# First expert matrix: VectorE and GpSimd in program order, with paced routing

## The chip, the cores and the metric

The kernel runs on one core of a Trainium2 chip. The metric is the device time of one execution in microseconds; the median of three runs before the change is 2098.88 us (2098.55 to 2100.28). The engines are named as in the profile: PE (TensorE), DVE (VectorE), ACT (ScalarE), POOL (GpSimd), SP (the DMA queues of SyncE).

## The reference, cut to what matters

Two transformer blocks for 256 tokens of width 1024. The change lies in the expert layer of the first block, which retrieves 16 single-neuron experts out of 128 x 128 for each of 8 heads:

```python
qh = (x_blk @ w_q).reshape(tc, PEER_HEADS, 2, PEER_HALF)
scores = jnp.einsum('thpc,hpnc->thpn', qh, skf)
s_top, i_top = lax.top_k(scores, PEER_TOPK)
cand = s_top[:, :, 0, :, None] + s_top[:, :, 1, None, :]
...
c_s, c_pos = lax.top_k(cand.reshape(tc, PEER_HEADS, PEER_TOPK * PEER_TOPK), PEER_TOPK)
g = jax.nn.softmax(c_s, axis=-1)
u = expert_u[e_idx]
v = expert_v[e_idx]
a = jax.nn.gelu(jnp.einsum('td,thkd->thk', x_blk, u), approximate=False)
return jnp.einsum('thk,thkd->td', g * a, v)
```

The kernel gathers nothing. It computes the product of every token with all 16384 rows of `expert_u` (the first matrix), and multiplies the result by gates that are zero for experts not chosen, before the product with `expert_v`.

## The kernel before, in words

**Order of the stages.** A projection gives the queries (`s_mode` over `w_q`, 16 steps), and each group of 4 of its output tiles is followed by the scores against the sub-keys (`q_evac`). Then `u_part(0, ...)` computes blocks 0 to 63 of the first matrix (128 experts each), `u_part(64, ...)` blocks 64 to 127, and two `v_part` calls the product with the second matrix. While the second half of the first matrix runs, the gates of the first half are built and applied; the gates of the second half run beside `v_part`.

**One block of the first matrix.** `blocks(j)` (line 760) takes the raw block, which a stream has loaded into one of 4 buffers, and transposes it on DVE (line 767) in two parts: the larger into an SBUF tile `ut` (640 columns for j < 64, else 768), the rest into a PSUM tile. `parted(j)` (line 770) splits the result into a rounded high part and the remainder: ACT copies both parts into `uhi` (line 774), then POOL subtracts for the larger part and DVE for the smaller (line 776, `ulo`). The tiles `whi`, `wlo` and `ut` have 3 buffers each. PE runs 24 matmuls per block (lines 247 to 249: eight chunks, three products), and ACT applies the Gelu (line 794). In `u_part` the split runs two blocks ahead of PE and the transpose three ahead.

**Routing.** The generator `chosen` loads and transposes the sub-keys (`sub_keys`), searches the best 16 of 128 scores 32 times (`tops`, `best`, lines 849 to 855: MAX8, FIND_INDEX8 and MATCH_REPLACE8 on DVE), then for each half of the tokens builds 64 candidate sums, searches 8 times in them, decodes positions and picks the indices by comparison (`routing`, lines 864 to 955; the pick steps are lines 912 to 921). Each `yield` is a place where the caller may go on with its own work. The query stage advances it by two yields per step (line 971 ff.), `u_part(0)` by 2.3 yields per block through `every`.

**Gates.** `hot(i)` (line 996) makes the one-hot tiles of 8 tokens: two comparisons (lines 1008 and 1011) and two products (line 1010) on DVE. `outer(i)` (line 1013) runs 16 small matmuls into PSUM (line 1018), `apply(i)` (line 1021) multiplies the expert results by them (line 1024, two instructions). `pipe(..., fine=True)` runs these three for 32 groups as three yields per step, and `u_part(64)` advances it by 1.7 yields per block.

**What sets the order.** Outside a `manual_schedule` block the framework's scheduler orders each engine's instructions when the program is built, starting from program order and letting what is ready go ahead. Inside such a block the named engines keep program order. Before the change neither half of the first matrix stands in such a block. Loads of raw blocks are issued from SP, ACT and, for j < 64, POOL (line 102). Waits between engines are semaphores that the framework places.

Of the kernel before, what the change touches and what calls it, by code (L numbers as in the profile page):

```python
# [9 lines left out]
F32 = mybir.dt.float32  # L10
# [4 lines left out]
ALU = mybir.AluOpType  # L15
# [141 lines left out]
def tile_kernel(ctx: ExitStack, tc: tile.TileContext, I, out, cst, dbg=None):  # L157
# [186 lines left out]
    adv = [0.0]  # L344

# [409 lines left out]
    with ExitStack() as pp:  # L755
# [14 lines left out]
        def parted(j, tr):  # L770
            hi = wpool.tile([P, D], F32R, tag="whi", name=f"uhi{j}", bufs=3)
            lo = wpool.tile([P, D], F32R, tag="wlo", name=f"ulo{j}", bufs=3)
            for _, c, x in tr:
                S.activation(hi[:, c], x, AF.Copy)  # L774
            for eng, c, x in tr:
                eng.tensor_tensor(lo[:, c], x, hi[:, c].bitcast(F32), op=ALU.subtract)  # L776
            return hi, lo

        def u_part(j0, trs, dst, bg, n):
# [18 lines left out]
            drain(bg)  # L798

        with ExitStack() as pr_:  # L800
# [58 lines left out]
            def tops(q):  # L859
                for e in range(4 * q, 4 * q + 4):  # L860
                    for t in range(2):
                        yield from best(top[t][:, e], ti[t][:, e], sco[t][:, e, :], e % 2)

            def routing():
# [3 lines left out]
                for t in range(2):  # L868
# [14 lines left out]
                    yield  # L883
                    for h in range(8):
                        yield from best(cs[:, h], cp[:, h], cand[:, h], True)
# [9 lines left out]
                    yield  # L895
# [3 lines left out]
                    yield  # L899
# [3 lines left out]
                    yield  # L903
# [3 lines left out]
                    yield  # L907
                    ix = R.tile([P, 2, P], F32, tag="ix", name=f"ix{t}")

                    for s in range(2):  # L910
# [3 lines left out]
                        yield  # L914
                        V.tensor_tensor(e, e, tf[:, s, :, None, :].to_broadcast([P, 16, 16, 8]), op=ALU.mult)
                        yield
                        V.tensor_tensor(e[:, 0:8], e[:, 0:8], e[:, 8:16], op=ALU.add)
                        yield
# [3 lines left out]
                        yield  # L922
                    for _ in range(3):
                        yield
# [4 lines left out]
                    yield  # L929
                    for s in range(2):  # L930
                        V.tensor_copy(ixt[s][:, ts], ps[:, s * P:(s + 1) * P])

# [6 lines left out]
                for _ in range(6):  # L939
                    yield  # L940
                V.tensor_reduce(sm, g, axis=AX.X, op=ALU.add)
                yield
# [3 lines left out]
                for _ in range(3):  # L946
                    yield
# [3 lines left out]
                yield  # L951
                V.tensor_scalar(ixt[2], ps[:, :T], GS, None, op0=ALU.mult)
                yield
                V.scalar_tensor_tensor(ixt[3], ps[:, :T], GS, ixt[2], op0=ALU.mult, op1=ALU.subtract)
                yield

            def chosen():
                yield from sub_keys()
                yield
# [32 lines left out]
        def gates(half, dst, H):  # L992
# [34 lines left out]
            yield from pipe(T // 8, (1, outer), (2, apply), (0, hot), fine=True)  # L1027
# [24 lines left out]
        with tc.tile_pool(name="hot", bufs=1) as H:  # L1052
            bgg = gates(0, a0, H)
            u_part(64, ahead, a1, bgg, 1.7)
# [6 lines left out]
            bgg = gates(1, a1, H)  # L1061
# [455 lines left out]
```

## Time and profile before

| what | value |
|---|---|
| median of three runs | 2098.88 us |
| profiled execution, its own time | 2100.21 us |
| its span | 2098.4 us |
| PE busy | 2015.3 us (96%) |
| DVE busy | 1484.0 us (71%) |
| ACT busy | 907.0 us (43%) |
| POOL busy | 448.3 us (21%) |
| mean granted clock of PE | 0.986 of full speed |

A busy PE is not a PE at its best: matmuls are pipelined, so the count of instructions in a stretch says more than the busy time. In the rows of windows further down, a row is a stretch, its length, and then for each of PE, PEld (weight loads), DVE, ACT and POOL the busy time and in brackets the number of instructions; behind them the granted clock, the DMA share and GB/s. Rows of a timeline are start, duration, engine, line, operation, tile written and tiles read; a bracket at the end is idle time before it and what ended it. Rows of waits are who waited for whom, the sum in us, how often, and the longest. Rows of groups are line, engine, operation, shapes and count, then the busy sum and the mean in ns of one.

### The profile page before, as it was taken

What the parts mean: (1) busy time and instruction counts of PE and PEld (TensorE: products, weight loads), DVE (VectorE), ACT (ScalarE), POOL (GpSimd) and SP (SyncE); (2) the same over time, 40 slices, a digit from 0 to 9 for tenths busy, and PEclk for the clock granted to TensorE, in tenths of its full rate; (3) what the DMA queues carried; (4) which work ended last, traced back from release to release, by engine and by line L of the source; (5) the groups of instructions that cost most, each with busy time, mean ns of one, the idle gap of its engine ahead of it and who ended that gap; (6) DMA issues with size and microseconds to landing.
All of it is one profiled execution on the core that took longest, in us unless ns stands there. A gap on an engine that the chain in (4) does not pass through costs nothing.

```text
span 2098.4 us, 33634 instructions
## 1 busy us (share of the span) xinstructions
PE 2015.3 (96%) x12513; PEld 1747.3 (83%) x12513; DVE 1484.0 (71%) x2664; ACT 907.0 (43%) x1537; POOL 448.3 (21%) x458
## 2 busy tenths in 40 slices
PE   8999998999999999999999998999999989899999
PEld 7898987999999888878887777877888878558997
DVE  4666699779999888879667758756532377766554
ACT  4565543544333444444454223322222267565443
POOL 0002665764455300010002211111000033300000
PEclk9999999999999999999999999999999999999999
DMA  6435564775555644468557645456532345115654
GB/s 221 141 121 194 159 161 131 195 176 139 137 142 141 201 161 158 157 226 292 194 186 243 216 158 186 157 190 218 176 101 90 119 141 157 52 61 151 181 186 146
DMA packets 181032, 344.18 MB, mean 164 GB/s; under 512 B 18412, under 2 KB 87684, under 8 KB 180868
## 3 DMA queue, kind: packets, MB, share of 16 engines
q1 hardware_dynamic: 138388, 254.44, 39.8%
q0 software_dynamic: 20512, 67.53, 10.3%
q10 hardware_dynamic: 21968, 20.06, 3.4%
q8 instruction: 98, 1.61, 0.3%
q14 instruction: 66, 0.54, 0.1%
HBM read 339.78 MB, written 2.18 MB: 163 GB/s over the span
## 4 chain that ended last, share of the span: by engine, by line
PE 69%; issue 10%; DVE 10%; POOL 5%; DMA 5%; ACT 1%; SPq 0%; POOLq 0%; DVEq 0%; ACTq 0%
PE acc L279 9%; PE acc L278 9%; PE acc L280 9%; PE acc L1045 5%; PE acc L1046 5%; PE acc L1049 5%; PE acc L312 4%; PE acc L313 4%; PE acc L315 4%; POOL ulo L776 4%; DMA mem<-in_mod_w_dram 2%; PE acc L249 2%; PE acc L247 2%; PE acc L248 2%; PE misc L1018 2%
## 5 line engine op out<-in xcount | busy, mean ns | idle before, releaser
L109 DVE TENSOR_TENSOR wlo<-raw,whi 128x1024 fp32r<-128x1024 f32 (+2 forms) x401 | 483.7, 1209 | 399.4 <-ACT whi L108 396.3
L108 ACT ACTIVATE whi<-raw 128x1024 fp32r<-128x1024 f32 (+1 forms) x412 | 429.8, 1046 | 660.5 <-PE acc L279 276.2
L278 PE MATMUL acc<-act,whi 128*128 128x512 f32 (+1 forms) x944 | 322.4, 343 | 3.1 <-DVE act L1089 3.1
L280 PE MATMUL acc<-act,wlo 128*128 128x512 f32 (+1 forms) x944 | 321.7, 341 | 2.6 <-DVE wlo L109 2.6
L279 PE MATMUL acc<-act,whi 128*128 128x512 f32 (+1 forms) x944 | 322.7, 342 | 1.6 <-DVE act L1090 1.6
L249 PE MATMUL acc<-x2h,ulo 128*128 128x256 f32 x1024 | 296.0, 289 | 17.7 <-DVE ulo L776 14.2
L247 PE MATMUL acc<-x2h,uhi 128*128 128x256 f32 x1024 | 294.8, 288 | 2.9 <-DVE ulo L776 2.5
L248 PE MATMUL acc<-x2l,uhi 128*128 128x256 f32 x1024 | 291.5, 285 | 0.0
L776 POOL TENSOR_TENSOR ulo<-ut,uhi 128x640 fp32r<-128x640 f32 (+1 forms) x128 | 224.3, 1763 | 162.1 <-ACT uhi L774 156.6
L249 PEld LDWEIGHTS acc<-x2h,ulo 128*128 128x128 f32 x1024 | 198.2, 194 | 25.0 <-DVE ulo L776 17.7
L278 PEld LDWEIGHTS acc<-act,whi 128*128 128x128 f32 x944 | 180.3, 192 | 31.0 <-DVE act L1089 4.0
L247 PEld LDWEIGHTS acc<-x2h,uhi 128*128 128x128 f32 x1024 | 198.6, 194 | 4.8 <-DVE ulo L776 4.8
L1045 PE MATMUL acc<-whi,g 128*128 128x512 f32 x512 | 202.6, 396 | 0.0
L1046 PE MATMUL acc<-wlo,g 128*128 128x512 f32 x512 | 199.9, 390 | 0.9 <-DVE wlo L109 0.9
L280 PEld LDWEIGHTS acc<-act,wlo 128*128 128x128 f32 x944 | 181.2, 192 | 22.8 <-DVE wlo L109 3.0
L279 PEld LDWEIGHTS acc<-act,whi 128*128 128x128 f32 x944 | 181.1, 192 | 21.5 <-DVE act L1090 2.4
L248 PEld LDWEIGHTS acc<-x2l,uhi 128*128 128x128 f32 x1024 | 198.3, 194 | 0.0
L774 ACT ACTIVATE uhi<-ut 128x640 fp32r<-128x640 f32 (+1 forms) x128 | 101.5, 793 | 223.8 <-DVE ut L767 169.7
L1049 PE MATMUL acc<-whi,g 128*128 128x512 f32 x512 | 157.8, 389 | 0.0
L496 DVE SCALAR_TENSOR_TENSOR mem<-mem,silu_c 128x1024 f32<-128x1024 f32 x84 | 106.5, 1281 | 18.9 <-DMA mem<-in_mod_w_dram 18.6
L767 DVE STREAM_TRANSPOSE ut<-raw 128x640 f32<-128x640 f32 (+1 forms) x128 | 114.5, 894 | 6.1 <-DMA raw<-in_peer_u_dram 3.7
L1046 PEld LDWEIGHTS acc<-wlo,g 128*128 128x128 f32 x512 | 96.2, 188 | 21.0 <-DVE wlo L109 2.3
(397 smaller groups left out, 3816.3 us busy)
## 6 DMA issues: line engine op xcount, KB each, us to landing
raw<-in_peer_v_dram SPq DMA_DIRECT2D x128, 512.0 KB, 3.3
raw<-in_peer_u_dram SPq DMA_DIRECT2D x320, 128.0 KB, 3.3
mem<-in_mod_w_dram POOLq DMA_DIRECT2D x64, 512.0 KB, 5.3
raw<-in_ffn_w_down_dram SPq DMA_DIRECT2D x50, 512.0 KB, 3.2
raw<-in_ffn_w_gate_dram SPq DMA_DIRECT2D x44, 512.0 KB, 4.4
raw<-in_ffn_w_up_dram SPq DMA_DIRECT2D x44, 512.0 KB, 3.8
raw<-in_w_in_dram SPq DMA_DIRECT2D x40, 512.0 KB, 3.8
raw<-in_peer_u_dram ACTq DMA_DIRECT2D x128, 128.0 KB, 3.4
```

The source lines that it names most:

```text
L108: a = self.nc.scalar.activation(hi, src, AF.Copy)
L109: b = (eng or self.nc.vector).tensor_tensor(lo, src, hi.bitcast(F32), op=ALU.subtract)
L247: mm(ps, lh, rh, start=first, stop=False)
L248: mm(ps, lh, rl, start=False, stop=False)
L249: mm(ps, ll, rh, start=False, stop=last)
L278: mm(ps[n][:, cs], hi[:, k - k0, c], xh[:, k, cs], start=first, stop=False)
L279: mm(ps[n][:, cs], hi[:, k - k0, c], xl[:, k, cs], start=False, stop=False)
L280: mm(ps[n][:, cs], lo[:, k - k0, c], xh[:, k, cs], start=False, stop=last)
L776: eng.tensor_tensor(lo[:, c], x, hi[:, c].bitcast(F32), op=ALU.subtract)
L1045: mm(ov[t][h], gh[:, ts], vh[:, 0, hs], start=j == 0, stop=False)
L1046: mm(ov[t][h], gh[:, ts], vl[:, 0, hs], start=False, stop=False)
L1049: mm(ov[t][h], gl[:, ts], vh[:, 0, hs], start=False, stop=j == P - 1)
```

## The change

- Both halves of the first matrix stand in a block that keeps DVE and POOL in program order. The first covers `u_part(0)` and the transposes of blocks 64 and 65, the second `u_part(64)`.
- In `u_part` a block first takes a piece of background work (routing or comparisons), then transposes block j+3, then splits block j+2, then takes late background work. POOL's subtraction gets a wait for the last DVE instruction ahead of the transposes (`latest`, `mark`).
- All blocks are divided 768 to 256 between POOL and DVE.
- Routing yields an estimated cost in us, and `budget` lets so much of it pass per call: 3.4 per step of the query stage from the fifth step on, 1.25 per block. A bare `yield` ends the current slice. The sub-keys are loaded in the first four steps, five yields each.
- The gates' three parts are called separately: `hot` ahead of the transposes in even blocks (twice in the first), `outer(i)` and `apply(i-1)` behind the split in odd ones. The gates of the second half keep `pipe`.

The diff, cut to its core:

```diff
+    def budget(per, gen):
+        due = per
+        for cost in gen:
+            due = min(due - cost, per) if cost else min(due, 0.0)
+            while due <= 0:
+                yield
+                due += per
...
-            c = (5 if j < 64 else 6) * P
+            c = 6 * P
...
+        def latest():
+            return next(i for i in reversed(nc.cur_bb.bb.instructions) if i.engine == V.engine)
...
-                eng.tensor_tensor(lo[:, c], x, hi[:, c].bitcast(F32), op=ALU.subtract)
+                a = eng.tensor_tensor(lo[:, c], x, hi[:, c].bitcast(F32), op=ALU.subtract)
+                if eng is G and after is not None:
+                    tc.add_manual_dep(a.ins, after.name, mybir.DependencyInfo(
+                        mybir.DependencyClass.Sync, mybir.DependencyReason.DATA), reason="the shared port")
...
-        def u_part(j0, trs, dst, bg, n):
+        def u_part(j0, trs, dst, bg, late=iter(())):
...
                 hi, lo = ahead.pop(0)
-                if j + 2 < j1:
-                    ahead.append(parted(j + 2, trs.pop(0)))
+                next(bg, None)
+                mark = latest()
                 if j + 3 < j1:
                     trs.append(blocks(j + 3))
-                advance(bg, n)
+                if j + 2 < j1:
+                    ahead.append(parted(j + 2, trs.pop(0), mark))
+                next(late, None)
...
-            def best(val, idx, x, last):
+            def best(val, idx, x):
+                one = 0.16 + x.shape[-1] / 1000
                 V.max(val[:, 0:8], x)
                 V.max_index(idx[:, 0:8], val[:, 0:8], x)
-                yield
+                yield 2 * one + 0.07
                 V.match_replace(out=x, in_to_replace=val[:, 0:8], in_values=x, imm_value=-3e38)
                 V.max(val[:, 8:16], x)
-                yield
+                yield 2 * one + 0.07
                 V.max_index(idx[:, 8:16], val[:, 8:16], x)
-                if last:
-                    yield
+                yield one + 0.07
...
-            ways = chosen()
+            first, ways = sub_keys(), chosen()
+            early_ways = budget(3.4, ways)
...
-                advance(ways, 2)
+                if i < 4:
+                    advance(first, 5)
+                else:
+                    next(early_ways, None)
...
-            bgr = every(1 / 2.3, ways)
...
-            u_part(0, ahead, a0, bgr, 1)
-            ahead = [blocks(64), blocks(65)]
+            with tc.manual_schedule(engines={V.engine, G.engine}):
+                u_part(0, ahead, a0, budget(1.25, ways))
+                ahead = [blocks(64), blocks(65)]
...
-            yield from pipe(T // 8, (1, outer), (2, apply), (0, hot), fine=True)
+            return hot, outer, apply
...
-            bgg = gates(0, a0, H)
-            u_part(64, ahead, a1, bgg, 1.7)
+            hot, outer, apply = gates(0, a0, H)
+            n = T // 8
+            def before():
+                hot(0)
+                for i in range(1, n):
+                    hot(i)
+                    yield
+                    yield
+            def late():
+                outer(0)
+                yield
+                for i in range(1, n + 1):
+                    if i < n:
+                        outer(i)
+                    apply(i - 1)
+                    yield
+                    yield
+            with tc.manual_schedule(engines={V.engine, G.engine}):
+                u_part(64, ahead, a1, before(), late())
...
-            bgg = gates(1, a1, H)
+            hot, outer, apply = gates(1, a1, H)
+            bgg = pipe(n, (1, outer), (2, apply), (0, hot), fine=True)
```

In `routing` the other steps yield costs too: 1.8 for the candidate sums, 0.8, 0.8, 0.6 and 0.7 for decoding the positions, 1.2, 1.2, 0.7 and 1.1 for each of the two picks, 0.5 for the copies of the indices, all of these once per half of the tokens, and 0.8 at the end; the waits for PE and ACT are bare yields.

## Rows read from the trace of the kernel before

**Rows 1.** Windows: stretch, length, busy us (instructions) of PE, PEld, DVE, ACT, POOL; clock.

```profile
271.10:479.20 208.10, 191.97 (x1545) 187.64 (x1544) 176.53 (x461) 94.48 (x196) 132.20 (x123) 0.99 0.64 160
479.20:715.50 236.30, 229.06 (x2050) 221.36 (x2051) 231.70 (x393) 91.56 (x195) 118.31 (x62) 0.99 0.58 144
...
380.00:470.00 90.00, 90.00 (x753) 90.00 (x752) 64.87 (x108) 43.12 (x93) 63.71 (x60) 1.00 0.75 186
...
290.00:358.00 68.00, 56.66 (x441) 53.51 (x439) 67.76 (x234) 25.04 (x53) 37.27 (x35) 1.00 0.50 133
...
474.00:483.00 9.00, 7.11 (x46) 6.75 (x45) 6.65 (x14) 6.36 (x10) 2.09 (x2) 0.81 0.19 49
...
240.00:265.00 25.00, 25.00 (x211) 25.00 (x210) 18.02 (x103) 11.22 (x19) 19.54 (x15) 1.00 0.59 161
```

**Rows 2.** Timeline of PE around a group of 16 gate products, second half.

```profile
564.11 0.28 PE L249 MATMUL acc<-x2h,ulo 128*128 128x256 f32 x1
564.23 1.15 PE L1018 MATMUL misc<-p,p 128*128 128x64 f16 x16
565.19 0.37 PE L247 MATMUL acc<-x2h,uhi 128*128 128x256 f32 x1
```

**Rows 3.** Waits from 271 to 716 us: who waited for whom, sum, times, longest.

```profile
PEld acc L249 <- DVE ulo L776: 17.7, 17, 2.2
...
PEld acc L249 <- POOL ulo L776: 6.2, 14, 1.3
```

**Rows 4.** Timeline of DVE in the second half: start, duration, what.

```profile
558.93 0.40 DVE L1008 TENSOR_TENSOR p<-ixt,iota 128x512 f16<-128x512 f16 x1
559.25 2.31 DVE L1011 TENSOR_TENSOR p<-ixt,iota 128x1024 f16<-128x1024 f16 x1
561.49 0.87 DVE L1010 TENSOR_TENSOR p<-p,ixt 128x512 f16<-128x512 f16 x2
...
564.49 1.90 DVE L1008 TENSOR_TENSOR p<-ixt,iota 128x512 f16<-128x512 f16 x1
566.31 0.68 DVE L1011 TENSOR_TENSOR p<-ixt,iota 128x1024 f16<-128x1024 f16 x1
```

**Rows 5.** Timeline of POOL in the same stretch.

```profile
557.19 3.83 POOL L776 TENSOR_TENSOR ulo<-ut,uhi 128x768 fp32r<-128x768 f32 x2 [3.47 <-ACT uhi L774]
564.27 1.84 POOL L776 TENSOR_TENSOR ulo<-ut,uhi 128x768 fp32r<-128x768 f32 x1 [3.25 <-ACT uhi L774]
```

**Rows 6.** Groups of DVE from 479 to 716 us: busy us, mean ns.

```profile
L767 DVE STREAM_TRANSPOSE ut<-raw 128x768 f32<-128x768 f32 x62 | 59.5, 960 | 0.1
...
L767 DVE STREAM_TRANSPOSE misc<-raw 128x256 f32<-128x256 f32 x64 | 26.8, 418 | 0.0
L776 DVE TENSOR_TENSOR ulo<-misc,uhi 128x256 fp32r<-128x256 f32 x64 | 25.5, 400 | 1.2 <-ACT uhi L774 1.1
...
L1024 DVE SCALAR_TENSOR_TENSOR a<-misc,a 128x256 f32<-128x256 f32 x64 | 23.5, 404 | 0.0
```

**Rows 7.** Timeline of DVE where PE is dense, first half.

```profile
414.56 0.56 DVE L776 TENSOR_TENSOR ulo<-misc,uhi 128x384 fp32r<-128x384 f32 x1 [1.09 <-ACT uhi L774]
415.03 0.83 DVE L767 STREAM_TRANSPOSE ut<-raw 128x640 f32<-128x640 f32 x1
```

**Rows 8.** Timeline of POOL in the same stretch.

```profile
413.95 1.58 POOL L776 TENSOR_TENSOR ulo<-ut,uhi 128x640 fp32r<-128x640 f32 x1 [0.81 <-ACT uhi L774]
415.47 0.56 POOL L102 DMA_DIRECT2D raw<-in_peer_u_dram  x1
```

**Rows 9.** Timeline of DVE in the query stage: searches.

```profile
234.31 0.28 DVE L849 MAX8 top<-sco 128x8 f32<-128x128 f32 x1
234.51 0.28 DVE L853 MAX8 top<-sco 128x8 f32<-128x128 f32 x1
...
240.07 0.28 DVE L852 MATCH_REPLACE8 sco<-top,sco 128x128 f32<-128x128 f32 x1
240.38 0.29 DVE L853 MAX8 top<-sco 128x8 f32<-128x128 f32 x1
```

More of the change, by code (lines that the diff above doesn't have):

```diff
@@ L798, in u_part @@
             drain(bg)
+            drain(late)
         with ExitStack() as pr_:
@@ L861, in tops @@
                     for t in range(2):
-                        yield from best(top[t][:, e], ti[t][:, e], sco[t][:, e, :], e % 2)
+                        yield from best(top[t][:, e], ti[t][:, e], sco[t][:, e, :])
             def routing():
@@ L882, in routing @@
                                         tv[:, :, 1, None, :nb].to_broadcast([P, 8, na, nb]), op=ALU.add)
-                    yield
+                    yield 1.8
                     for h in range(8):
-                        yield from best(cs[:, h], cp[:, h], cand[:, h], True)
+                        yield from best(cs[:, h], cp[:, h], cand[:, h])
                     ab = R.tile([P, 2, 16, 8], U32, tag="ab", name=f"ab{t}")
@@ L894, in routing @@
                     V.tensor_copy(c, cpk)
-                    yield
+                    yield 0.8
                     V.tensor_scalar(a, ab[:, 0], -1.0, 0.0, op0=ALU.add, op1=ALU.max)
@@ L906, in routing @@
                     V.tensor_tensor(b, c, f, op=ALU.subtract)
-                    yield
+                    yield 0.7
                     ix = R.tile([P, 2, P], F32, tag="ix", name=f"ix{t}")
@@ L913, in routing @@
                                         i16[:, :, None, :].to_broadcast([P, 16, 16, 8]), op=ALU.is_equal)
-                        yield
+                        yield 1.2
                         V.tensor_tensor(e, e, tf[:, s, :, None, :].to_broadcast([P, 16, 16, 8]), op=ALU.mult)
-                        yield
+                        yield 1.2
                         V.tensor_tensor(e[:, 0:8], e[:, 0:8], e[:, 8:16], op=ALU.add)
-                        yield
+                        yield 0.7
                         for n in (4, 2):
@@ L921, in routing @@
                         V.tensor_tensor(ix[:, s].rearrange("p (h k) -> p k h", h=8), e[:, 0], e[:, 1], op=ALU.add)
-                        yield
-                    for _ in range(3):
-                        yield
+                        yield 1.1
+                    yield
                     ps = misc()
@@ L938, in routing @@
                 tc.keep_in_program_order(S.activation(g, g, AF.Exp))
-                for _ in range(6):
-                    yield
+                yield
+                yield
+                yield
                 V.tensor_reduce(sm, g, axis=AX.X, op=ALU.add)
-                yield
                 V.reciprocal(sm, sm)
@@ L945, in routing @@
                     V.tensor_tensor(g[:, t], g[:, t], sm[:, t, :, None].to_broadcast([P, 8, 16]), op=ALU.mult)
-                for _ in range(3):
-                    yield
+                yield
                 ps = misc()
@@ L951, in routing @@
                 yield
+                yield
                 V.tensor_scalar(ixt[2], ps[:, :T], GS, None, op0=ALU.mult)
-                yield
                 V.scalar_tensor_tensor(ixt[3], ps[:, :T], GS, ixt[2], op0=ALU.mult, op1=ALU.subtract)
-                yield
+                yield 0.8
             def chosen():
-                yield from sub_keys()
-                yield
                 for q in range(4):
@@ L1052, in tile_kernel @@
         with tc.tile_pool(name="hot", bufs=1) as H:
-            bgg = gates(0, a0, H)
-            u_part(64, ahead, a1, bgg, 1.7)
+            hot, outer, apply = gates(0, a0, H)
[4 more added lines that the diff above has]
+                    hot(i)
+                    yield
+                    yield
+            def late():
+                outer(0)
+                yield
+                for i in range(1, n + 1):
+                    if i < n:
+                        outer(i)
+                    apply(i - 1)
+                    yield
+                    yield
+            with tc.manual_schedule(engines={V.engine, G.engine}):
+                u_part(64, ahead, a1, before(), late())
             ov = [[acc() for _ in range(2)] for _ in range(2)]
```

7 lines of the change are left out of this document (4 added, 3 removed).

## The prediction

> **What bounds the kernel now.** I read the windows first, stage by stage. The first half of the experts' first matrix (blocks 0 to 63) runs from 271.1 to 479.2 us, the second (64 to 127, beside the gates) from 479.2 to 715.5 us; look at the counts behind PE, not at its busy time [rows 1]. From 380 to 470 us PE issues 753 instructions in 90 us, 0.12 us each, and waits for nothing; from 290 to 358 us it issues 441 in 68 us, where 0.12 us would allow 567. In that second stretch DVE is busy 67.76 of 68 us; in the first only 64.87 of 90. So the first half is bound by DVE early and by PE late. In the second half DVE is busy 231.7 of 236.3 us throughout.
>
> One block is 24 products (8 chunks by 3), 24 x 0.12 = 2.88 us; I call that a slot. The PE timeline gives the price of one group of 16 gate products: the product ahead starts at 564.11, the one behind at 565.19, 1.08 us where 0.12 is usual, so 0.96 us [rows 2]. There are 32 groups in the second half. If PE never waited, the first half would take 64 x 2.88 = 184.3 us and the second 184.3 + 32 x 0.96 = 215.0 us. They take 208.1 and 236.3: **23.8 and 21.3 us are lost, 45.1 us in all**. That is the most that this change can give back in its own stages. The waits name who ends them: the longest of PE's are for DVE's and GpSimd's subtraction, line 776 [rows 3].
>
> Why DVE is full in the second half shows in two timelines side by side. The comparison of line 1011 takes 0.68 us at 566.31 but 2.31 at 559.25, and that of line 1008 takes 1.90 at 564.49 [rows 4]. GpSimd's subtractions run from 557.19 to 561.02 and from 564.27 to 566.11 [rows 5]: each slow comparison starts inside one and ends 0.3 to 0.5 us behind its end. It stands still as long as GpSimd subtracts. The transposes do not: 0.96 us in the mean in this stage, and 0.83 for the smaller form right beside a GpSimd subtraction [rows 6 to 8].
>
> **The change, part by part.** *Gates in program order, GpSimd behind the comparisons.* DVE's work per two blocks, without collisions: one comparison of line 1008 at 0.40, one of 1011 at 0.68, two products of 1010 at 0.43 (the unstalled ones of [rows 4]), and from the group means two applications at 0.40, two large transposes at 0.96, two small ones at 0.42, two subtractions at 0.40: 6.30 us [rows 4, 6]. PE needs 2 x 2.88 + 0.96 = 6.72. Now it is 231.7 / 32 = 7.24 of DVE, above PE; with the collisions gone it is below, and PE sets the pace. Does the wait only move the collision? GpSimd starts behind the last comparison of an even block, takes 1.84 [rows 5], and has until the next even block's comparisons, one period of 6.72 less about 1.95 for the comparisons themselves, 4.8 us later, for two subtractions of 3.7 in all. That fits, with 1.1 us left. Behind the waiting instruction on GpSimd stand only the following subtraction (and in the first half a DMA issue); lo is wanted two slots later, and a delay of 1.95 us is under one slot. Bounds for what stays lost in the second half: 0, and all 21.3. I take 3.
>
> *The outer products one slot behind their comparisons* (outer in the next odd block, apply two blocks on): the same number of instructions; cover is the slot between. Nothing, or once, at the first group, the 1.95 us of one set of comparisons. At the border of the halves PE issues only 46 instructions in 9 us, 9 - 46 x 0.12 = 3.5 us lost, some of it at a granted clock of 0.81 (part of the 45.1) [rows 1], because routing ends there; with a budget it ends some four blocks earlier. But two comparison sets (2 x 1.95 us) now stand ahead of block 64's transposes. Between 0 and 3.5, I take 2.
>
> *Routing by budget.* The diff's own costs: a search over 128 scores 1.65 us, over 64 candidates 1.33. In the query stage 12 steps x 3.4 = 40.8 us, 24 of 32 searches. Left for the first half: 8 x 1.65 + 2 x (1.8 + 8 x 1.33 + 2.9 + 8.4 + 0.5) + 0.8 = 62.5 us, at 1.25 per block over by block 60. Transposes and subtractions per block: 0.96 + 0.42 + 0.40 = 1.78, x 64 = 114 us [rows 6]. Sum 176.4 us against PE's 184.3: PE sets the pace, with 8 us to spare. In a dense slot DVE waits 1.09 us for ScalarE ahead of its subtraction [rows 7]; routing and transposes of the next block stand behind that wait, but they need nothing of it but the engine, and DVE works a block ahead.
>
> What could eat the 8 us: GpSimd's subtraction starts at 413.95, DVE's at 414.56, 0.6 us later, and ends at 415.1 [rows 7, 8]. With 768 columns GpSimd lasts 1.84, to 415.8; routing that starts at 415.1 would meet 0.7 us of it. Of routing, what is built like the stalled comparisons of [rows 4] are chiefly the 16 pick steps: 0 to 16 x 0.7 = 11 us, so 0 to 3 us beyond the margin, and unevenness on top. I take 3 lost of the 23.8.
>
> *Program order costs DVE interleaving.* In the query stage two searches run mixed: MAX8 at 234.31 and 234.51, 0.20 apart; a search alone has 0.31 from its replacement to the MAX8 that needs it [rows 9]. The sum above has the dependent price already (1.65). [...]
>
> *GpSimd takes 768 columns in the first half too*: 1.58 becomes 1.84 us, with a DMA issue of 0.56 [rows 5, 8] 2.40 of 2.88 per slot. Hidden beside PE, two slots ahead of use. DVE's part falls from 384 columns to 256; that is in the 1.78.
>
> *Query stage.* The sub-keys come in four steps instead of eight. PE is full there (25.00 of 25) and DVE has 7 us idle in 25 [rows 1]. The 24 searches at 1.65 are 39.6 us in some 37; mixed, at 1.65 - 4 x 0.11 = 1.21, they are 29, and DVE's order is free here. Between 0 and 6, I take 0.
>
> **Sum.** 45.1 - 3 - 2 - 3 = 37 us. The profiled execution took 2100.2 us (span 2098.4 and 1.8 around it): 2063.2. The median of the runs, 2098.9, is 1.3 below the profiled one: **2062 us**. PE-bound in both halves.
>
> **The rivals.** *First half stays DVE-bound*: program order, dependent searches and pick collisions fill the 8 us and more, and PE goes on waiting for line 776. For it: the margin is 4%, and 62.5 is the diff's own figure. Against: a whole slot of lead between subtraction and use. It keeps 20 us of the 23.8: gain 45.1 - 20 - 5 = 20, 2079 us. *The collision only moves*: the wait keeps GpSimd from starting early, but nothing keeps a comparison from starting while GpSimd still subtracts. For it: 1.1 us of room per pair. It keeps 18 of the 21.3: gain 45.1 - 18 - 5 = 22, 2077 us. *Slower: head of line.* DVE in program order stands at its subtraction for ScalarE's copy (1.09 us, [rows 7]); if transposes and routing behind it do not run a block ahead, the wait adds to the work: 1.09 + 1.78 + 62.5 / 64 = 3.85 x 64 = 246 us and 1.09 + 6.30 / 2 = 4.24 x 64 = 271, in place of 208 and 236: +73, 2172 us. It decides where a block's transposes end less than a slot before ScalarE needs them. Against it: blocks are transposed three ahead. *The order stays as it was*, because the marks lie where the scheduler put things anyway: 2099.
>
> **How the numbers follow.** Forecast 0.62 (own range 2055 to 2072: all regained, to twice the residue and a little), first half 0.17, moved collision 0.11, head of line 0.05, nothing 0.05. About 0.2% (4 us) is what a measurement of this kernel can tell from no change. Faster 0.62 + 0.17 + 0.11 = 0.90, same 0.05, slower 0.05. The range goes from all but 1 us regained, 2055, to just past the two rivals, 2081.
>
> **What would show it.** Right: DVE under 90% busy in the second half, line 1011 near 0.68 us in the mean, line 776 on GpSimd near 1.85; some 250 PE instructions per 30 us from 290 to 358 us as well; halves of about 187 and 220 us. Wrong: PE waiting for line 776 in the pick steps (first rival), comparisons still near 2 us (second), DVE idle for ScalarE for more than 1 us per block while PE waits (third). A query stage ending later than 271 us would be a cost that I set at nothing.

## The result, and the profile after

The kernel became **slower**: 2113.32 us in the median of 4 runs (2109.61 to 2118.76), against 2099.58 for the kernel before (4 runs, 2098.55 to 2101.66). The ratio is 1.006, with a 95% interval of 1.0043 to 1.0077. The forecast of 2062 and its whole range, 2055 to 2081, lie below it. The profiled execution took 2109.61 us, its span 2107.8.

**Where the time went.** The windows of the kernel after, columns as in [rows 1]:

```profile
272.50:477.60 205.10, 189.56 (x1561) 186.78 (x1560) 172.40 (x465) 94.63 (x201) 151.55 (x125) 0.99 0.63 171
477.60:728.50 250.90, 224.00 (x2037) 218.53 (x2034) 194.24 (x380) 85.15 (x189) 115.11 (x62) 0.99 0.50 131
380.00:470.00 90.00, 83.85 (x689) 82.66 (x688) 74.76 (x184) 42.54 (x90) 66.94 (x54) 1.00 0.62 168
290.00:358.00 68.00, 68.00 (x565) 67.64 (x564) 64.33 (x193) 32.11 (x71) 54.53 (x47) 1.00 0.65 179
```

Against [rows 1] the first half begins 1.4 us later and takes 3.0 less (208.1 to 205.1), the second takes 14.6 more (236.3 to 250.9), and what follows, 3.6 less (1382.9 to 1379.3). Together +9.4, the difference of the two spans. The early stretch of the first half was cured as forecast: 565 PE instructions from 290 to 358 us where there were 441. The late stretch, dense before, got worse: 689 from 380 to 470 us where there were 753. And in the second half DVE's busy time fell from 231.7 to 194.2 us. DVE was relieved of 37 us, and the stage grew.

The groups of DVE in the second half, columns as in [rows 6], show that the collisions are mostly gone:

```profile
L1033 DVE TENSOR_TENSOR p<-ixt,iota 128x512 f16<-128x512 f16 x32 | 28.8, 903 | 0.0
...
L791 DVE TENSOR_TENSOR ulo<-misc,uhi 128x256 fp32r<-128x256 f32 x62 | 25.6, 412 | 53.7 <-ACT uhi L789 53.7
...
L1036 DVE TENSOR_TENSOR p<-ixt,iota 128x1024 f16<-128x1024 f16 x33 | 22.6, 684 | 0.0
```

The large comparison (now line 1036) takes 0.684 us in the mean, its unstalled 0.68 of [rows 4]. Only the small one (line 1033) still meets half a microsecond of GpSimd, 0.90 against 0.40. What is new is the last column of the subtraction: DVE stands idle there for 53.7 us, for ScalarE. It was 1.2 us in [rows 6].

The waits from 480 to 728 us, in the form of [rows 3]:

```profile
ACT a L816 <- DVE misc L777: 137.5, 26, 5.7
POOL ulo L791 <- ACT uhi L789: 68.4, 30, 3.1
POOL ulo L791 <- DVE p L1036: 63.5, 31, 3.8
DVE ulo L791 <- ACT uhi L789: 53.7, 29, 2.6
PEld L1043 <- DVE p L1036: 31.8, 25, 1.6
PE misc L1043 <- DVE p L1036: 26.8, 25, 1.4
```

In the second half TensorE no longer waits for subtractions, as in [rows 3], but for the comparison ahead of each group of gate products (line 1043). In the first half, from 272 to 478 us, it still waits for GpSimd's:

```profile
PEld acc L249 <- POOL ulo L791: 12.1, 11, 1.7
```

In the list of the second half the longest row is the strange one: ScalarE waits 137.5 us, some 5.3 each time, with a Gelu (line 816) behind a *transpose* of DVE. A Gelu reads a PSUM result and needs no transpose. Something ahead of it on ScalarE's queue does.

**One period of the second half.** ScalarE, start, duration, what (ACTq marks DMA issues, waiting time included in the duration):

```profile
601.39 1.84 ACTq L102 DMA_DIRECT2D raw<-in_peer_u_dram  x2
603.28 0.38 ACT L816 ACTIVATE a<-acc 128x256 f32<-128x256 f32 x1 [5.33 <-DVE misc L777]
603.56 0.84 ACT L789 ACTIVATE uhi<-ut 128x768 fp32r<-128x768 f32 x1
604.30 0.38 ACT L789 ACTIVATE uhi<-misc 128x256 fp32r<-128x256 f32 x1
...
611.62 0.84 ACT L789 ACTIVATE uhi<-ut 128x768 fp32r<-128x768 f32 x1
```

DVE in the same period:

```profile
600.05 0.97 DVE L777 STREAM_TRANSPOSE ut<-raw 128x768 f32<-128x768 f32 x1
...
602.46 0.42 DVE L777 STREAM_TRANSPOSE misc<-raw 128x256 f32<-128x256 f32 x1
604.71 0.42 DVE L791 TENSOR_TENSOR ulo<-misc,uhi 128x256 fp32r<-128x256 f32 x1 [1.82 <-ACT uhi L789]
605.05 0.74 DVE L1049 SCALAR_TENSOR_TENSOR a<-misc,a 128x256 f32<-128x256 f32 x2
605.71 0.91 DVE L1033 TENSOR_TENSOR p<-ixt,iota 128x512 f16<-128x512 f16 x1
...
607.45 0.69 DVE L1036 TENSOR_TENSOR p<-ixt,iota 128x1024 f16<-128x1024 f16 x1
608.05 0.97 DVE L777 STREAM_TRANSPOSE ut<-raw 128x768 f32<-128x768 f32 x1
...
610.47 0.42 DVE L777 STREAM_TRANSPOSE misc<-raw 128x256 f32<-128x256 f32 x1
```

And TensorE's groups of gate products:

```profile
600.19 1.17 PE L1043 MATMUL misc<-p,p 128*128 128x64 f16 x16 [1.09 <-DVE p L1036]
...
608.20 1.16 PE L1043 MATMUL misc<-p,p 128*128 128x64 f16 x16 [1.04 <-DVE p L1036]
```

Read as a loop. The transpose of block 97's larger part ends at 600.05 + 0.97 = 601.02. Its copy on ScalarE could start then, but starts at 603.56. Ahead of it ScalarE has two issues of raw loads (line 102). The second fills, for block 102, the buffer that block 98 is transposed out of (there are four buffers), so it has to wait for the transposes of block 98, which end at 602.46 + 0.42 = 602.88. Behind the copies comes DVE's subtraction (604.71, after standing still for 1.82 us). DVE keeps program order, so its applications, its comparisons (to 608.14) and the next transposes (to 610.89) stand behind that subtraction; behind the transposes stands the next pair of loads, and behind these the next copy, at 611.62. From copy to copy it is 8.06 us per pair of blocks, and TensorE's groups follow at the same pace, 8.01 us apart, where they need 6.72. This is the loop that sets the stage: no engine is full in it.

In the first half ScalarE's queue has the same shape at the slow places: two loads at 424.84, a Gelu at 427.80 after 5.53 us of idle time, the copies behind it. Such pairs of loads also stand at 276.98, 363.38, 368.42 and 375.99, and beside or just behind the five places blocks take 3.6 to 4.8 us, from their first product to that of the next block, instead of 2.88. (Pairs at 308.78 and 456.63 cost nothing.)

Who put the loads there? ScalarE is not named in the new blocks, so the framework's scheduler still orders its queue. In the kernel before, in the stretch of [rows 4], the same queue has one load per block, and it does not wait (0.32 us):

```profile
563.35 0.85 ACT L774 ACTIVATE uhi<-ut 128x768 fp32r<-128x768 f32 x1 [1.41 <-DVE ut L767]
563.76 0.32 ACTq L102 DMA_DIRECT2D raw<-in_peer_u_dram  x1
564.10 0.36 ACT L774 ACTIVATE uhi<-misc 128x256 fp32r<-128x256 f32 x1
```

Why the scheduler now puts two loads ahead of a Gelu and the copies, no run shows.

### The profile page after: what moved, and what is told of

Read it like the earlier page. It is cut to its first block, busy times and chain, and to the rows that moved or that the text cites. A ratio compares the mean times of both kernels' runs of the same rounds, so it can differ in the third digit from the quotient of the medians.

```text
span 2107.8 us, 33675 instructions
## 1 busy us (share of the span) xinstructions
PE 2004.7 (95%) x12513; PEld 1741.8 (83%) x12513; DVE 1444.5 (69%) x2664; ACT 900.1 (43%) x1537; POOL 459.7 (22%) x458
## 4 chain that ended last, share of the span: by engine, by line
PE 66%; DVE 11%; issue 9%; DMA 8%; POOL 2%; ACT 2%; SPq 1%; ACTq 0%; DVEq 0%; POOLq 0%
PE acc L278 9%; PE acc L279 9%; PE acc L280 9%; PE acc L1070 5%; PE acc L1071 5%; DMA raw<-in_peer_u_dram 5%; PE acc L1074 5%; PE acc L312 5%; PE acc L313 5%; PE acc L315 5%; DVE ut L777 2%; PE misc L1043 2%; SPq L102 1%; DMA mem<-in_mod_w_dram 1%; DVE misc L777 1%
## 5 line engine op out<-in xcount | busy, mean ns | idle before, releaser
L791 POOL TENSOR_TENSOR ulo<-ut,uhi 128x768 fp32r<-128x768 f32 x128 | 237.0, 1853 | 182.7 <-ACT uhi L789 95.8
L789 ACT ACTIVATE uhi<-ut 128x768 fp32r<-128x768 f32 x128 | 108.1, 844 | 82.5 <-DVE ulo L791 44.2
L777 DVE STREAM_TRANSPOSE ut<-raw 128x768 f32<-128x768 f32 x128 | 123.2, 963 | 3.6 <-DMA raw<-in_peer_u_dram 3.3
L816 ACT ACTIVATE a<-acc 128x256 f32<-128x256 f32 x128 | 48.1, 376 | 181.6 <-DVE misc L777 150.4
```

The costliest lines, as they stand in the source:

```text
L791: a = eng.tensor_tensor(lo[:, c], x, hi[:, c].bitcast(F32), op=ALU.subtract)
```

## The experiments

All of them start from the kernel after. Ratios are against runs of the kernel before on the same chip; its medians there lie between 2099.3 and 2103.3 us, so a few us between two experiments can be the chip's.

**ScalarE in program order too.** The theory to test: the order of ScalarE's queue is the whole loss of the second half.

```diff
-            with tc.manual_schedule(engines={V.engine, G.engine}):
+            with tc.manual_schedule(engines={V.engine, G.engine, S.engine}):
```

in both places.

> The changed kernel with ScalarE also in program order in both blocks (one name more in each set of engines). Theory 1 (ScalarE's order: its queue, ordered when the program is built, holds the issue of a raw load that waits for VectorE's transposes, and Gelus, ahead of copies that could already run; VectorE in program order stands at its subtraction until the copy comes): the second half falls from 250.9 us to 215 to 225, the first from 205 to 187 to 197, the time to 2063 to 2085. Theory 2 (VectorE's comparisons come late by its own work, and the outer products right behind them stop TensorE): second half stays at 245 to 251, time within 8 us of the changed kernel. Theory 3 (GpSimd's wait for the mark makes ulo late): the same as theory 2.

Measured: **2072.37 us** (4 runs, 2071.32 to 2074.71), ratio 0.986 (0.9841 to 0.9878). 41 us less than after, and both halves lie where theory 1 put them. The windows of the two halves:

```profile
273.90:469.70 195.80, 186.72 (x1555) 185.90 (x1556) 176.63 (x465) 101.45 (x202) 151.81 (x124) 0.99 0.66 177
469.70:689.10 219.40, 217.90 (x2039) 216.36 (x2036) 195.21 (x381) 95.45 (x190) 116.23 (x65) 0.99 0.60 151
```

DVE does the same work (195.2 us busy), the stage is 31.5 us shorter. ScalarE's timeline now has one load per block, behind that block's Gelu and ahead of its copies:

```profile
600.28 0.39 ACT L816 ACTIVATE a<-acc 128x256 f32<-128x256 f32 x1 [1.89 <-PE acc L249]
600.44 0.32 ACTq L102 DMA_DIRECT2D raw<-in_peer_u_dram  x1
600.86 0.85 ACT L789 ACTIVATE uhi<-ut 128x768 fp32r<-128x768 f32 x1 [0.19 <-DMA raw<-in_peer_u_dram]
```

The waits from 500 to 680 us:

```profile
ACT a L816 <- PE acc L249: 89.9, 53, 2.5
POOL ulo L791 <- ACT uhi L789: 79.7, 51, 2.4
DVE ulo L791 <- ACT uhi L789: 15.8, 26, 0.9
...
POOL ulo L791 <- DVE p L1036: 2.0, 1, 2.0
```

ScalarE waits for TensorE now, as it should when TensorE sets the pace, and TensorE has no row. The groups of gate products start at 596.17 and 602.96, 6.79 apart. GpSimd's wait for the comparisons, the mark of the change, comes last once in this stretch.

**The loads off ScalarE's queue.** The same theory from the other side: leave ScalarE's order free, but give it no raw loads of the first matrix.

```diff
-    two, three = [nc.sync] * 3 + [nc.scalar], [nc.sync, nc.sync, nc.scalar, nc.gpsimd]
+    two, three = [nc.sync] * 4, [nc.sync, nc.sync, nc.sync, nc.gpsimd]
```

`two` names the queues of blocks 64 to 127, `three` those of blocks 0 to 63 and also of the query weights, so the edit moves a quarter of each of those loads as well.

> The changed kernel with the fourth piece of each raw block of the first matrix issued from SyncE's queue, not ScalarE's. Theory 1: the wait for the transposes leaves ScalarE's queue; Gelus may still stand ahead of copies, so the second half falls to 218 to 238 us and the time to 2070 to 2100. Theories 2 and 3: second half 245 to 251, time within 8 us of the changed kernel. If SyncE's queue is itself what is late, slower.

Measured: 2072.09 us (2 runs), ratio 0.9856 (0.9833 to 0.9879), the same as with program order. Second half 218.8 us, first 192.3; inside the first half, block 0 and the border with the second apart, no block takes more than 3.0 us. The query stage ended 6.3 us later (its last product starts at 275.7 instead of 269.4), which took the shorter first half back. Since the query weights' loads had moved too, this is not the price of the blocks' loads alone. So a second run moved only the loads of blocks 64 to 127:

```diff
-    two, three = [nc.sync] * 3 + [nc.scalar], [nc.sync, nc.sync, nc.scalar, nc.gpsimd]
+    two, three = [nc.sync] * 4, [nc.sync, nc.sync, nc.scalar, nc.gpsimd]
```

> The changed kernel with the fourth piece issued from SyncE's queue for blocks 64 to 127 alone (ScalarE keeps its own order and its loads in the first half). Theory 1, per half: the second half is cured, 216 to 226 us between the first blocks, the first keeps its slots of 4.4 to 4.8 us and 203 to 207 us; time 2075 to 2092. If what helped in the second experiment lay in the first half or in the query stage: second half stays above 240.

Measured: 2075.58 us (2 runs), ratio 0.9869 (0.9829 to 0.9908). Its windows:

```profile
272.50:474.70 202.20, 190.76 (x1560) 188.21 (x1560) 172.42 (x465) 94.78 (x201) 151.64 (x125) 0.99 0.64 173
474.70:691.80 217.10, 216.88 (x2037) 215.34 (x2034) 186.62 (x380) 88.09 (x189) 116.01 (x63) 1.00 0.54 151
```

The half whose loads were moved is cured (250.9 to 217.1), the half whose loads stay on ScalarE keeps nearly all of its loss (205.1 to 202.2, against 192.3 where they were moved; of the 2.9 us nearly all is in block 63, at the border). With the first run this shows what the loss needs: neither the order of DVE and GpSimd nor ScalarE's freedom alone costs the time, but both together with loads on ScalarE's queue, and that only where the loads come out ahead of the copies (an experiment further down has all three and 221.4 us). One thing these runs do not part: without the loads the scheduler also ordered ScalarE's copies and Gelus anew, block by block instead of in pairs. That it is the load that waits is read from the trace of the kernel after (601.39 to 603.23).

**Is the mark to blame?** A rival: GpSimd's wait for the comparisons makes its subtraction late.

```diff
-                if eng is G and after is not None:
+                if False:
```

> The changed kernel without GpSimd's wait for the mark (program order of VectorE and GpSimd kept). Theory 3: GpSimd starts earlier, second half 220 to 235 us. Theories 1 and 2: no gain; comparisons meet subtractions again, line 1036 (comparison of 1024) rises from 0.68 us to over 1 us in the mean, second half 245 to 265.

Measured: 2176.12 us (2 runs), ratio 1.0351 (1.0327 to 1.0375): some 60 us *worse* than after. The halves take 224.3 and 293.8 us. The rival falls, but the second half is far over what the other theories gave (245 to 265), and it is not line 1036 that collides: it stays at 0.68 us. The group of the products on DVE from 500 to 790 us:

```profile
L1035 DVE TENSOR_TENSOR p<-p,ixt 128x512 f16<-128x512 f16 x64 | 68.4, 1071 | 2.0
```

Two of them in DVE's timeline:

```profile
560.61 2.45 DVE L1035 TENSOR_TENSOR p<-p,ixt 128x512 f16<-128x512 f16 x2
```

And GpSimd in the same stretch:

```profile
560.47 1.85 POOL L791 TENSOR_TENSOR ulo<-ut,uhi 128x768 fp32r<-128x768 f32 x1 [0.17 <-ACT uhi L789]
```

The products collide now (1.07 us in the mean, 0.43 with the mark), and DVE's standing still lengthens the same loop: 41 us more of line 1035, 43 us more in the second half. Then the same edit on top of ScalarE in program order:

> ScalarE in program order as in the first experiment, and GpSimd without its wait for the mark. Theory A (the 63 us that the kernel without the mark lost came through ScalarE's order, which the mark had changed; with ScalarE in order GpSimd waits for ScalarE's copy, not for the mark): within 6 us of the first experiment (2072), second half 216 to 222. Theory B (the wait itself keeps VectorE's comparisons from standing behind a subtraction, 1.2 to 1.5 us per pair of blocks): second half 235 to 262, time 2090 to 2117.

Measured: 2089.21 us (5 runs), ratio 0.9941 (0.9918 to 0.9964). Neither theory has it whole: the second half does as theory A says, the time nearly as theory B does (2090 to 2117). The second half does not care (219.5 us, against 219.4): with ScalarE in order its copies come at a time that keeps GpSimd clear by itself. The first half takes 212.3 instead of 195.8. There routing meets the subtractions: the two conversions of positions (line 894) between 360 and 470 us take 2.80 us in the mean, one of them 4.99 and the other 0.60; with the mark the mean is 1.31 (2.03 and 0.60):

```profile
L894 DVE CAST tf<-ti 128x128 f16<-128x128 uint32 x2 | 5.3, 2798 | 0.0
```

So with ScalarE in order the mark is worth some 15 us, all in the first half. (Of the 16.5 between the two runs, 1.4 are block 0, which takes 4.6 or 6.1 us also in versions that are alike there.)

**The outer products one block later.** If TensorE only stands for the comparison, giving it a block more should do.

```diff
-                outer(0)
-                yield
-                for i in range(1, n + 1):
-                    if i < n:
-                        outer(i)
-                    apply(i - 1)
+                for i in range(n):
+                    outer(i)
                     yield
+                    if i:
+                        apply(i - 1)
                     yield
+                apply(n - 1)
```

> The changed kernel with each group of outer products one block later (in the even block that also makes the next comparisons). Theory 2: TensorE no longer waits for line 1036 (58.6 us of waits now), second half 218 to 230. Theory 1: the loop of two blocks on VectorE (6.2 us of work and 1.85 of waiting for ScalarE's copy) is untouched, a pair keeps 7.8 to 8.1 us, second half 243 to 252; TensorE waits for ulo or uhi in place of line 1036. Theory 3: as theory 1.

Measured: 2085.16 us (2 runs), ratio 0.9918 (0.9895 to 0.9941). The second half fell to 221.4 us, the first stayed at 205.1. That is the number of theory 2, and theory 1 missed it. But the run does not separate the theories, since in its trace ScalarE's order changed as well, to one load per block; against theory 2 speak the two experiments ahead, where the outer products stayed in place and the half was cured. It does show that the first half's loss has nothing to do with the gates.

**Program order in the first half alone.** The second half without its block, the mark and the order of the calls kept.

```diff
-            with tc.manual_schedule(engines={V.engine, G.engine}):
+            with ExitStack():
                 u_part(64, ahead, a1, before(), late())
```

> The changed kernel with the program-order block of the second half taken away (the order of calls and the mark stay). Theory 1 (a VectorE that keeps program order stands still for a copy that ScalarE's order delays): with VectorE free to go on with other work the second half falls to 222 to 242 us, time 2085 to 2105; first half as in the changed kernel, 203 to 207. If program order of VectorE is not part of the loop: second half 245 to 255, time as the changed kernel.

Measured: 2082.63 us (2 runs), ratio 0.99 (0.9868 to 0.9932). Halves 200.2 and 225.0, the first below its forecast: block 63, at the border, takes 3.8 us instead of 9.2. DVE is busy 223.6 of the 225.0 us, and the group of the large comparison says why:

```profile
L1036 DVE TENSOR_TENSOR p<-ixt,iota 128x1024 f16<-128x1024 f16 x30 | 68.3, 2276 | 0.0
```

With a free DVE the collision stays even with the mark, since the comparisons move. The mark removes it only together with program order. But a colliding DVE that may reorder beats one in order behind a ScalarE that isn't: 225.0 against 250.9.

**Pieces that did not matter.** Each on top of ScalarE in program order (2072.37). The first half divided 640 to 384 as before:

```diff
-            c = 6 * P
+            c = (5 if j < 64 else 6) * P
```

> ScalarE in program order, and the first half divided 640 to 384 as before. VectorE per block 0.83 + 0.55 + 0.56 = 1.94 us in place of 1.78, 10 us more over the half, and its sum with routing 187 us, over TensorE's 184.3. If VectorE's sum decides: first half 199 to 208 in place of 195.8, time 2075 to 2084. If TensorE has the lead to absorb it: within 3 us of 2072.

Measured: 2074.0 us (4 runs), ratio 0.9857 (0.9837 to 0.9877), first half 196.1. Fewer searches per step of the query stage:

```diff
-            early_ways = budget(3.4, ways)
+            early_ways = budget(2.8, ways)
```

> ScalarE in program order, and 2.8 in place of 3.4 us of routing per step of the query stage. In the first experiment block 0 starts 2.8 us later than before the change and the next block 1.7 us later still, 4.5 us. If the searches ahead of block 0's transposes on VectorE are that cost: block 0 starts at 270 to 272 us, 2 to 4.5 us regained, and up to 3 given back where routing now ends later: time 2067 to 2073. If not: start unchanged, time 2071 to 2078.

Measured: 2072.83 us (4 runs), ratio 0.9871 (0.9855 to 0.9888). Block 0 starts at 273.2 as against 274.1, but takes 6.1 us instead of 4.6, and the time is the same. (Block 0 also takes 6.1 us in other versions with 3.4, so the edit need not be the reason.)

One set of comparisons per even block from the first block on, never two, with the outer products one block behind them:

```diff
-                hot(0)
-                for i in range(1, n):
+                for i in range(n):
                     hot(i)
...
-                outer(0)
                 yield
-                for i in range(1, n + 1):
-                    if i < n:
-                        outer(i)
-                    apply(i - 1)
+                for i in range(n):
+                    outer(i)
+                    if i:
+                        apply(i - 1)
                     yield
                     yield
+                apply(n - 1)
```

> ScalarE in program order, and block 64 no longer preceded by two sets of comparisons: comparisons of group i in block 64+2i, outer products one block later. At the border of the halves block 63 to 64 takes 11.1 us and the next 4.8 in the first experiment, 9 over the floor; TensorE waits 7.1 us there for line 1036. If that wait is the cost: block 64 starts when its ulo is there, 4 to 6 us earlier, time 2064 to 2070; the rest of the second half unchanged. If the split of blocks 64 and 65 behind the Gelu of block 63 is the whole cost: no change, 2070 to 2074.

Measured: 2077.65 us (4 runs), ratio 0.9879 (0.9858 to 0.99). The first half ended 4.6 us sooner after its start (191.2), the second took 228.2 instead of 219.4: block 64 takes 7.1 us instead of 4.8, and a set of comparisons saved at the border comes back at the end, where block 126 takes 6.1 us and the product with the second matrix starts later. 4 to 5 us lost in all; neither case of the expectation came.

**The border between the halves.** With ScalarE in order the dearest place left was here. Windows of that kernel, columns as in [rows 1]:

```profile
460.00:464.00 4.00, 1.88 (x16) 1.68 (x14) 0.00 (x0) 1.50 (x4) 0.20 (x1) 1.00 0.62 158
464.00:467.00 3.00, 0.00 (x0) 0.00 (x0) 2.35 (x4) 2.01 (x4) 3.00 (x2) 0.68 0.55 149
467.00:469.70 2.70, 0.74 (x13) 0.75 (x14) 2.63 (x5) 0.00 (x0) 0.56 (x1) 0.50 0.02 6
469.70:472.00 2.30, 2.30 (x17) 2.30 (x15) 2.27 (x5) 0.00 (x0) 1.07 (x1) 0.52 0.03 7
```

The copies of blocks 64 and 65 stand in program order behind the Gelu of block 63, and DVE is idle for 5.3 us ahead of its subtraction (464.03); two sets of comparisons then stand ahead of block 66's subtraction. The edit lets `u_part(0)` transpose three and split two blocks beyond its end, as inside a half:

```diff
+            end = j1 if j0 else j1 + 3
...
-                if j + 3 < j1:
+                if j + 3 < end:
                     trs.append(blocks(j + 3))
-                if j + 2 < j1:
+                if j + 2 < end:
```

> ScalarE in program order, and blocks 64 to 66 transposed, 64 and 65 split, inside the loop of the first half as every other block, not behind its end. At the border 11.1 + 4.8 us stand for two blocks in the first experiment, floor 6.7. If the split behind the Gelu of block 63 holds the first comparisons up: 4 to 7 us less there, time 2064 to 2070. If the comparisons themselves hold it (they still stand ahead of block 64's outer products): 0 to 2 us less, time 2069 to 2074.

Measured: **2063.28 us** (4 runs, 2061.34 to 2068.55), ratio 0.9828 (0.9808 to 0.9848). The best version. Its windows:

```profile
274.10:464.10 190.00, 187.97 (x1554) 187.32 (x1555) 178.07 (x467) 100.19 (x199) 150.53 (x124) 0.99 0.66 179
464.10:682.70 218.60, 217.06 (x2040) 215.52 (x2037) 193.97 (x380) 96.75 (x193) 117.38 (x66) 1.00 0.61 155
...
464.00:467.00 3.00, 3.00 (x31) 3.00 (x29) 2.40 (x6) 1.39 (x3) 2.89 (x2) 1.00 0.82 213
```

The slots of blocks 63 and 64 went from 11.1 and 4.8 us to 3.9 and 3.9, which is their floor: each has a group of gate products, so 3.85, and the two 7.7 where the expectation has 6.7. To ask whether the first two sets of comparisons still cost something, they were moved into blocks 61 and 62, with routing ended ahead of them:

```diff
+            def ready():
+                for _ in range(61):
+                    yield
+                drain(ways)
+                hot(0)
+                yield
+                hot(1)
+                yield
...
-                u_part(0, ahead, a0, budget(1.25, ways))
+                u_part(0, ahead, a0, budget(1.25, ways), ready())
```

> As the kernel with the border closed, and the first two sets of comparisons made in blocks 61 and 62, behind the routing. Both causes at the border gone: two blocks there in 7 to 8.5 us, time 2062 to 2067. If the border is held by something else (the release of the routing's memory, the change of ScalarE's table): no more gain than the kernel with the border closed.

Measured: 2065.62 us (4 runs), ratio 0.9838 (0.9822 to 0.9854). No gain that can be told from none: the first two sets of comparisons cost nothing any more.

## Why the prediction was wrong

**The step that failed** is the cost of DVE's wait for ScalarE's copy, taken as nothing. It stands in the sentence on the dense slot: DVE waits 1.09 us for ScalarE ahead of its subtraction [rows 7], and "routing and transposes of the next block stand behind that wait, but they need nothing of it but the engine, and DVE works a block ahead". It costed the wait at nothing, because it asked what the work *behind* the wait needs. It did not ask who, on the engine waited for, needs that work: ScalarE's load issue needs the transposes that stand behind DVE's wait, and ScalarE's copy, which ends the wait, stands behind the load. In the second half the sum, 6.30 us of DVE against 6.72 of PE, has no term for the wait at all. The runs showed DVE standing there for 53.7 us and a pair of blocks at 8.06 us in place of 6.72; with ScalarE in order, or without loads on its queue, the half took 219.4 and 217.1 us instead of 250.9. In the kernel before, DVE could go on with other work; with DVE free again in the second half alone, that half took 225.0. The new blocks name V and G only; the third engine of the loop, S, kept the scheduler's order. The description of the kernel has "Loads of raw blocks are issued from SP, ACT and, for j < 64, POOL"; of POOL's issue the sum took account, of ScalarE's not.

**The rival that came true** is "slower: head of line", given 0.05 and 2172 us. Its mechanism, DVE standing at its subtraction for ScalarE, is the right one. Its price was too high: it put the full 1.09 us and all of DVE's work in series for every block, 271 us for the second half. Measured was 8.06 per pair, 250.9 in all, and in the first half 205.1 against its 246. Its sign, DVE idle for ScalarE for more than 1 us per block, was set a little too high: 53.7 / 64 = 0.84. Its deciding point (transposes ending less than a slot ahead) was not what decided; what did was a DMA issue.

**The other steps, one by one:**
- *TensorE's floor, 184.3 and 215.0 us*: right. In the best version the halves take 190.0 and 218.6, and nearly every slot is at 2.88, every pair at 6.80.
- *Collisions gone, GpSimd's two subtractions fit*: right but for half a microsecond per pair on line 1033. DVE's work per pair was put at 6.30 us; its busy time is 194.2 / 32 = 6.07, which counts overlapping ends of instructions once, as the sum of means does not.
- *First half bound by TensorE with 8 us to spare*: right once ScalarE's queue is in order. DVE's sum was put at 176.4 us and is 172.4 in the kernel after. The kernel after loses 20.8 us here (6.3 of them at the border), about what the first rival keeps (20), but to ScalarE's loads and not to a full DVE. In the best version the residue, 190.0 - 184.3 = 5.7, was taken as 3; 3.2 of it is block 0, and 1.0 the first group of gate products, which falls ahead of block 64.
- *Border, taken as 2 between 0 and 3.5*: mis-sized. In the kernel after, the slots of blocks 63 and 64 take 9.2 and 5.5 us instead of 3.85 each, 7.0 lost. The edge that I left out is that the copies of blocks 64 and 65, all but the first, come only behind the Gelu of block 63 (471.60). And the two sets of comparisons stand ahead of the transposes of block 67, not of block 64.
- *Query stage at nothing*: its end is nearly where it was (the last product starts at 269.4, before at 269.0). But block 0 starts 1.5 us later and blocks 0 and 3 take 4.68 and 4.49 us, 2.95 and 2.88 before, together 4.8 for which the sum has nothing. Block 3's part belongs to ScalarE's loads (276.98): with ScalarE in order it takes 2.88. For block 0, GpSimd's timeline:

```profile
270.10 0.55 POOL L102 DMA_DIRECT2D raw<-in_peer_u_dram  x1 [3.80 <-DVE misc L777]
272.15 0.55 POOL L102 DMA_DIRECT2D raw<-in_peer_u_dram  x1 [1.50 <-DVE misc L777]
272.71 3.62 POOL L791 TENSOR_TENSOR ulo<-ut,uhi 128x768 fp32r<-128x768 f32 x2
```

Its first subtraction stands behind two load issues that wait for transposes; in the kernel before it came at 266.32, ahead of the loads. It looks like ScalarE's trouble on a smaller scale. That is argued from the trace only: no run moved those loads.
- *Program order costs interleaving of searches, 768 columns are hidden*: the second is right, since the run with 640 columns moved nothing. The first no run tests by itself; the run with fewer searches per step moved nothing either.

The sum forecast a gain of 37 us. The version with ScalarE in order and the border closed has it: its span is 35.8 us shorter than that of [rows 1], 18.1 + 17.7 from the halves, 3.0 given back at the start and 3.0 gained behind 682.7, for a reason that no run shows. The number was that of another kernel, two edits away from this one, and that it is met so closely there is in part luck: the two 3.0 cancel, and neither was in the sum.

## What to carry to other kernels

Before taking an engine's freedom to reorder, follow each of its new head-of-line waits to the engine that ends it, and list *everything* ahead of the releasing instruction on that engine's queue, DMA issues included; if one of these waits for work behind the first wait, there is a loop, and its length per iteration is the new pace, whatever the busy shares say. Here three ways out worked: the third engine in program order too (219.4 us), its loads on a queue that computes nothing (217.1), and, less well, DVE left free (225.0). And look what else a list of queues serves: with the query weights' loads moved too, the query stage ended 6.3 us later. Where a pipeline runs ahead of its consumer, let it run ahead across the border of two stages as well.

## What the runs showed of the hardware

- **GpSimd's subtraction stops more of DVE than the comparisons.** The products of line 1035 (0.43 us alone) took 2.45 for two beside it. A conversion (0.45 to 0.62 alone) that began at 373.19, 0.44 us ahead of a subtraction, in the run without the mark and with ScalarE in order, took 4.99 and ended 0.3 behind the next subtraction. The large transposes stayed at 0.96 us with and without the mark. The Trainium skill (GPSIMD Engine Reference, section "1. Specifications") says that GpSimd shares its SBUF interfaces with VectorE, and that DVE instructions with two SBUF inputs or in a 2-port mode contend with it. The trace agrees for the comparisons and products, which read two SBUF tensors; what mode the conversion ran in, no row shows.
- **A waiting DMA issue stops the engine that issues it.** ScalarE was idle for some 5.3 us per pair behind its loads. Where its loads did not wait (0.32 us each, in the kernel before and with ScalarE in order), they did no such harm. The loads of blocks 64 to 127 from SP alone cost the second half nothing (217.1 us). The Trainium skill (Trainium Kernel Development and Optimization, section "Key Constraints") says that issuing from several engines only saves issue time, as the transfers share the same DMA engines; the second half agrees. With the loads of blocks 0 to 63 and of the query weights moved as well, the query stage ended 6.3 us later; how much of that is issue time, no row shows.
- **A gap in TensorE's work is paid twice.** At the border of the version with ScalarE in order TensorE issued nothing from 464 to 467 us, and the granted clock fell to 0.50, the 1.2 GHz level, until 472: block 64 took 4.8 us instead of 3.9. With the gap closed the clock stayed at 1.00. In the run without the mark it was 0.89 over the whole second half.
